# End of the feed-forward block: column groups of 6, 8, 8 and a second half that starts with the weights still on chip

## The chip, the cores and the metric

The kernel runs on one core of one Trainium2 chip. Its time is the device time of one execution in microseconds (us); lower is better. The core's engines run side by side and each works through its own queue in order: TensorE (PE in the rows, PEld for its weight loads), VectorE (DVE), ScalarE (ACT), GpSimd (POOL), and SyncE (SP), which here only issues DMAs.

## The reference

The program is a trunk of four layers over 512 token columns of width 1024: 256 context columns ("half 0") and 256 latent columns ("half 1"). Each layer has a mixer (kinds 0, 1, 2, 0) and then a feed-forward block (FFN). Before and after each there is an RMS norm with scales and shifts ("mods") that come from a small matrix product of a condition vector with `w_mod`. What the change touches is the FFN:

```python
def conv_ffn(h, w_in, conv_w, conv_b, w_out):
    u = dwconv_centred(h @ w_in, conv_w, conv_b)
    a, v = jnp.split(u, 2, axis=-1)
    return (jax.nn.silu(a) * v) @ w_out

h_l = rmsnorm(lat, norm_g[i, 2]) * (1.0 + m_l[4]) + m_l[3]
lat = lat + m_l[5] * rmsnorm(conv_ffn(h_l, ...), norm_g[i, 3])
```

`h @ w_in` gives 2 x 2816 rows, that is 22 pairs (a, v) of 128 rows; `w_out` takes the 22 gated rows of 128 back to 1024, that is 8 output groups of 128. In the last layer only half 1 is computed.

## The kernel before, in words

**Products in three matmuls.** An f32 product is made from split operands: `hi` is the value rounded to the matmul's format, `lo` the remainder. `mm3` (L680) issues three matmuls per k-chunk of 128: hi x hi (L688), lo x hi (L689), hi x lo (L690). Weights come as raw tiles `wraw` of up to 128 x 2048 by DMA and are split on the chip: ACT writes `whi` (L112, two instructions), DVE writes `wlo` (L115, two or more). `Stream` holds the list of weight tiles in program order. There are two raw buffers and two split buffers. `get` hands out the next split tile and, with `lead` 1, puts the split of the following one on a list; `mm3` issues one step of that list after every second k-chunk. Each split puts one raw load on SP's queue.

**The FFN** (`ffn`, L863). The 22 pairs are worked in three column groups, `FSPLIT`. In each group the pairs come first: a pair is 2 x 8 k-chunks of matmuls on `h` (48 matmuls of 512 columns), then ACT and DVE make the gated values `gh`, `gl` (lines 883 to 895). Then come the 8 output groups m = 0..7, each summing over the pairs of that column group only; two output groups share one weight tile ("fo", 256 x pairs columns). The results of the three column groups are added up in `y`. The first two output groups first run all pairs but the last three (`FS`) each, so that the gates of the last pair have time. In the last column group the output groups run once per half, with 256 columns: first all eight for half 0, then all eight for half 1, and before the change the four weight tiles are loaded and split again for half 1.

**What runs in between.** After the last output group of a half, `chain` (L492) is started: sum of squares (matmuls with `ones`, L446), square root on ACT, reciprocal on DVE, the update of `x`, a second norm, and the next layer's `h`. It is a generator; `mm3` advances it at k = 2 and k = 6 (`FT`). The chain of half 0 thus runs beside the output groups of half 1, and its instructions stand between theirs in every queue. Two further jobs are spread over the FFN. `s5_prep` (L1459, layers 0 and 1) prepares matrices of layer 2's mixer with small products (L1510) and, two advances later, transposes (L1538); it also advances with the k-chunks. `mod_block` (L300) makes a block of mods from two `wm` tiles (matmuls L314, then L383) and then has the next block's two tiles loaded (`mod_load`, L290); only one block is held on chip. `mod_slot` (L403) is called before each pair and after every second output group of the first two column groups, and runs a block when the count of slots passed says that one is due:

```python
m[3] += 1
if self.mod_nd < m[0] + min(m[1], -(-m[1] * m[3] // m[2])):
    self.mod_block()
```

So the last slot of a column group (after m = 7) and the first slot of the next (before its first pair) have no matmul between them. In layer 2 the mods are made on DVE instead.

**The FFN ends.** Layers 0 and 2 end as described (`tail` 0). In layer 1 the next mixer is of kind 2; its last pair is also done once per half (`tail` 1). Layer 3 has half 1 alone, so all its matmuls there have 256 columns.

Of the kernel before, what the change touches and what calls it, by code (L numbers as in the profile page):

```python
# [13 lines left out]
KINDS = (0, 1, 2, 0)  # L14
D = 1024
NK = 8
T = 512
NJ = 22
FSPLIT = (8, 7, 7)
FHEAD, FTAIL = (2, 1)  # L20
DM = 1
CW = (1, 8, 6)
# [24 lines left out]
FS = 3  # L47
# [34 lines left out]
class Stream:  # L82
# [10 lines left out]
    def add(self, key, ap, n):  # L93
        self.plan.append((key, ap, n))
# [57 lines left out]
class Kern:  # L152
# [688 lines left out]
    def plan_ffn(self, l, halves):  # L841
        tail = FTAIL if l < 3 and KINDS[l + 1] == 2 else 0
        add = self.ws.add
        fi = lambda j: add(("fi", l, j), self.a["f_w_in"][l * NJ + j], 2048)
        fo = lambda p, nj: [add(("fo", l, p, m), self.a[f"fo{p}"][l * 4 + m], 256 * nj) for m in range(NK // 2)]
        j0 = 0
        for p, nj in enumerate(FSPLIT):
            n0 = j0
            if p == 0 and len(halves) == 2:
                for j in [*range(FHEAD)] * (1 if FHEAD == 2 else 2):  # L850
                    fi(j)
                n0 = FHEAD
            last = p == len(FSPLIT) - 1
            t0 = j0 + nj - (tail if last else 0)
            for j in range(n0, t0):
                fi(j)
            for _ in range(2 if last and len(halves) == 2 else 1):
                for j in range(t0, j0 + nj):
                    fi(j)
                fo(p, nj)  # L860
            j0 += nj

    def ffn(self, l, halves, nxt):  # L863
        nc, tc = self.nc, self.tc
        both = len(halves) == 2
        allh = None if both else halves[0]
        tail = FTAIL if l < 3 and KINDS[l + 1] == 2 else 0
        cw0, cb0 = VEC["cw"][0] + l * 132, VEC["cb"][0] + l * 44
        rng = lambda half: (0, T) if half is None else RNG[half]
        with tc.tile_pool(name="ffn", bufs=1) as fp:  # L870
# [27 lines left out]
            def pair(j, half, G, ticks, w=None, defer=False):  # L898
                if w is None:
                    w = self.pairw(("fi", l, j))[0]  # L900
                ps = [self.proj(w[c], half, ticks) for c in range(2)]
                if j not in G:
                    G[j] = [fp.tile([128, T], F32R, name=n, bufs=max(FSPLIT)) for n in ("gh", "gl")]
                a, b = rng(half)
                run = lambda: act(j, ps, G[j][0][:, a:b], G[j][1][:, a:b])
                if defer:
                    return run
                run()

            j0 = 0  # L910
            for p, nj in enumerate(FSPLIT):
                G = {}
                n0 = j0
                if p == 0 and both:
                    ws = []
                    for half in halves:
                        for j in range(FHEAD):
                            if FHEAD == 2 and half == 0:
                                self.ws.lead = 1 - j
                                ws.append(self.pairw(("fi", l, j))[0])  # L920
                                self.ws.lead = 1
                            post = pair(j, half, G, None, ws[j] if ws else None,
                                        DF and half == 0 and j == FHEAD - 1)
                            if FHEAD == 2 and half and j == 0:
                                self.ws.prefetch()
                        self.drain(DM if half == 0 else 0)
                        if post:
                            post()
                    n0 = FHEAD
                if p == 0 and 2 in KINDS and l < 2:  # L930
                    self.bg = self.s5_prep(fp, 8 * l, 8 * l + 8)
                t0 = j0 + nj - (tail if p == len(FSPLIT) - 1 else 0)
                self.von, self.vpool = l in VO, fp
                for j in range(n0, t0):
                    if l not in VO:
                        self.mod_slot()
                    pair(j, allh, G, (3, 7))
                last = p == len(FSPLIT) - 1
                if last:
                    self.von = False  # L940
                self.cols = last and nxt is None
                if last and nxt is not None:
                    self.mod_until(nxt[0], 0)
                elif last:
                    self.mod_until(l, 5)
                for half in (halves if last else (allh,)):
                    a, b = rng(half)
                    for j in range(t0, j0 + nj):
                        pair(j, half, G, None)
                    self.flush()  # L950
                    for m in range(NK):
                        if m == 6 and last and nxt is not None and half == halves[-1] and KINDS[nxt[0]] == 2:
                            self.ws.lead = 0
                        if m % 2 == 0:
                            w = [t[:, :256 * nj].rearrange("p (c k m) -> p c k m", c=2, k=nj)
                                 for t in self.ws.get(("fo", l, p, m // 2))]
                        if m == 6 and last and nxt is not None and half == halves[-1] and KINDS[nxt[0]] == 2:
                            self.s5_pre = [self.s5_load("wraw", self.s5_h(i)) for i in range(2)]
                        g = lambda k: [G[j0 + k][z][:, a:b] for z in range(2)]
                        ticks = FT if last else (2, nj - 1)  # L960
                        if m < 2 and FS:
                            if m == 0:
                                two = [self.acc()[:, :b - a] for _ in range(2)]
                                for i in range(2):
                                    self.mm3(two[i], [t[:, i] for t in w], g, nj - FS, ticks, True, False)
                            ps = two[m]
                            self.mm3(ps, [t[:, m, nj - FS:] for t in w], lambda k: g(nj - FS + k), FS,
                                     [k - nj + FS for k in ticks], False, True)
                        else:
                            ps = self.acc()[:, :b - a]  # L970
                            self.mm3(ps, [t[:, m % 2] for t in w], g, nj, ticks)
                        if not last and m % 2 and l not in VO:
                            self.mod_slot()
                        if last and m == 3:
                            nc.scalar.activation(self.np_.tile([128, 8], F32, name="rs", bufs=4)[:, :1], self.epsc, AF.Sqrt)
                        y, ps = self.Y(m, half, ps)
                        if p == 0:
                            nc.scalar.activation(y, ps, AF.Copy)
                        else:
                            nc.vector.tensor_tensor(y, ps, y, op=ADD)  # L980
                        if last:
                            self.sq_add(("y", half), m, y)
                    if last:
                        self.drain()
                        self.gens.append(self.chain(l, 3, half, nxt))
                j0 += nj
# [943 lines left out]
```

## Time and profile before

| what | value |
|---|---|
| time, median of 3 runs | 2921.64 us (2917.19 to 2922.3) |
| the profiled execution's own time | 2920.22 us |
| its span, first to last instruction | 2918.4 us |
| busy: PE, DVE, ACT, POOL | 94%, 68%, 44%, 7% of the span |
| granted TensorE clock, mean | 0.969 of full speed |

The span is nearly all of the execution: 1.8 us lie outside it. A row's idle time, in square brackets, is the time for which the engine stood still just before the instruction, with the one that released it behind the arrow. In the windows view PEclk is the granted clock as a share of full speed: 1.00 is 2.4 GHz and 0.50 is 1.2 GHz.

### The profile page before, as it was taken

To read this page: it belongs to the slowest core of one execution; us is meant where nothing else is said; L and a number is where in the kernel's file an instruction comes from. 1 tells how busy PE (TensorE), PEld (TensorE's weight loads), DVE (VectorE), ACT (ScalarE), POOL (GpSimd) and SP (SyncE) were. 2 spreads that over 40 slices of the span, in tenths; PEclk is the share of its full clock that TensorE was granted. 3 is DMA by queue.
4 is the path that set the end of the run, shared out by engine and by line. 5 is a ranking of instruction groups with operands and counts; after the bars stand their busy time and mean duration, and the time that the engine had idled before them with its cause. 6 is when DMAs were issued, how large, how long until landed. Compare 5 with 4: busy or idle time off the path is not lost.

```text
span 2918.4 us, 53174 instructions
## 1 busy us (share of the span) xinstructions
PE 2740.2 (94%) x21814; PEld 2267.2 (78%) x21814; DVE 1992.1 (68%) x4405; ACT 1290.1 (44%) x2154; POOL 194.9 (7%) x192
## 2 busy tenths in 40 slices
PE   8999998999999999899999877989999989998998
PEld 5787776877788777777777745778888877887998
DVE  5775768766557655687564766378687876777776
ACT  4333334634335545553333565454332463433554
POOL 0000001122101000012110010010000010000000
PEclk9999999999999999999999988899999999999999
DMA  6232232355524343235555387433334453332553
GB/s 260 88 112 93 102 99 76 131 178 178 172 93 150 104 164 109 102 123 191 199 180 178 125 228 251 150 120 132 137 124 147 143 179 126 120 124 95 186 182 124
DMA packets 127043, 421.26 MB, mean 144 GB/s; under 512 B 36048, under 2 KB 55760, under 8 KB 102096
## 3 DMA queue, kind: packets, MB, share of 16 engines
q1 hardware_dynamic: 118608, 391.64, 39.5%
q0 software_dynamic: 5472, 23.07, 2.3%
q8 instruction: 172, 2.82, 0.4%
q10 hardware_dynamic: 2720, 3.15, 0.3%
q14 instruction: 71, 0.58, 0.1%
HBM read 392.78 MB, written 29.23 MB: 145 GB/s over the span
## 4 chain that ended last, share of the span: by engine, by line
PE 72%; DVE 16%; ACT 5%; DMA 3%; issue 2%; SPq 1%; POOL 0%; ACTq 0%; DVEq 0%; POOLq 0%
PE acc L688 19%; PE acc L689 18%; PE acc L690 17%; DVE wlo L115 3%; PE aux L314 2%; PE aux L1103 2%; PE acc L724 2%; PE acc L726 1%; PE acc L725 1%; DVE bc L462 1%; DVE y L561 1%; ACT whi L112 1%; PE aux L1143 1%; PE aux L383 1%; DVE y L520 1%
## 5 line engine op out<-in xcount | busy, mean ns | idle before, releaser
L688 PE MATMUL acc<-h,whi 128*128 128x512 f32 (+1 forms) x2368 | 868.3, 367 | 24.8 <-ACT h L574 15.3
L689 PE MATMUL acc<-h,whi 128*128 128x512 f32 (+1 forms) x2368 | 842.7, 356 | 19.4 <-DVE h L581 17.0
L690 PE MATMUL acc<-h,wlo 128*128 128x512 f32 (+1 forms) x2368 | 837.8, 354 | 2.3 <-DVE wlo L115 2.3
L115 DVE TENSOR_TENSOR wlo<-wraw,whi 128x512 fp32r<-128x512 f32 (+5 forms) x674 | 601.7, 920 | 153.0 <-ACT whi L112 152.6
L688 PEld LDWEIGHTS acc<-h,whi 128*128 128x128 f32 x2368 | 458.6, 194 | 94.1 <-ACT h L574 18.2
L689 PEld LDWEIGHTS acc<-h,whi 128*128 128x128 f32 x2368 | 458.9, 194 | 80.0 <-DVE h L581 24.3
L112 ACT ACTIVATE whi<-wraw 128x1024 fp32r<-128x1024 f32 (+3 forms) x496 | 479.5, 1014 | 66.6 <-PE acc L689 51.7
L690 PEld LDWEIGHTS acc<-h,wlo 128*128 128x128 f32 x2368 | 458.8, 194 | 62.1 <-DVE wlo L115 3.2
L688 PE MATMUL acc<-gh,whi 128*128 128x256 f32 (+1 forms) x872 | 294.7, 338 | 8.6 <-ACT gh L894 8.6
L689 PE MATMUL acc<-gl,whi 128*128 128x256 f32 (+1 forms) x872 | 287.2, 329 | 0.8 <-DVE gl L895 0.7
L690 PE MATMUL acc<-gh,wlo 128*128 128x256 f32 (+1 forms) x872 | 287.1, 329 | 0.0
L883 ACT ACTIVATE u<-acc,vec 128x512 f32<-128x512 f32 (+1 forms) x190 | 129.6, 692 | 254.5 <-PE acc L690 254.3
L886 DVE SCALAR_TENSOR_TENSOR u<-acc,vec,u 128x510 f32<-128x510 f32 (+1 forms) x190 | 122.2, 643 | 113.2 <-ACT u L883 113.0
L688 PEld LDWEIGHTS acc<-gh,whi 128*128 128x128 f32 x872 | 164.8, 189 | 25.6 <-ACT gh L894 9.0
L689 PEld LDWEIGHTS acc<-gl,whi 128*128 128x128 f32 x872 | 164.7, 189 | 16.8 <-DVE gl L895 1.7
L690 PEld LDWEIGHTS acc<-gh,wlo 128*128 128x128 f32 x872 | 164.6, 189 | 15.9
L1074 DVE TENSOR_TENSOR FB<-FB,P 128x256 f32<-128x256 f32 x384 | 145.2, 421 | 31.9 <-PE aux L1103 29.3
L887 DVE SCALAR_TENSOR_TENSOR u<-acc,vec,u 128x510 f32<-128x510 f32 (+1 forms) x190 | 123.1, 648 | 6.7
L724 PE MATMUL acc<-whi,h 128*128 128x256 f32 x384 | 115.2, 300 | 2.2 <-ACT whi L112 1.2
L894 ACT ACTIVATE gh<-u 128x512 fp32r<-128x512 f32 (+1 forms) x95 | 52.3, 551 | 144.1 <-DVE u L893 144.1
L726 PE MATMUL acc<-wlo,h 128*128 128x256 f32 x384 | 110.0, 287 | 4.1 <-DVE wlo L115 4.1
L725 PE MATMUL acc<-whi,h 128*128 128x256 f32 x384 | 109.7, 286 | 0.0
(298 smaller groups left out, 3957.2 us busy)
## 6 DMA issues: line engine op xcount, KB each, us to landing
wm<-in_w_mod SPq DMA_DIRECT2D x192, 512.0 KB, 5.3
wraw<-in_f_w_in SPq DMA_DIRECT2D x89, 1024.0 KB, 4.9
wraw<-in_fo SPq DMA_DIRECT2D x44, 896.0 KB, 4.6
wraw<-in_a_qz SPq DMA_DIRECT2D x18, 1024.0 KB, 4.9
wraw<-in_a_zg SPq DMA_DIRECT2D x18, 1024.0 KB, 4.9
wraw<-in_fo SPq DMA_DIRECT2D x16, 1024.0 KB, 4.9
wraw<-in_a_v SPq DMA_DIRECT2D x15, 1024.0 KB, 4.9
wraw<-in_c_glu SPq DMA_DIRECT2D x12, 1024.0 KB, 4.8
```

The source lines that it names most:

```text
L112: nc.scalar.activation(hi[:, a:b], r[:, a:b], AF.Copy)
L115: nc.vector.tensor_tensor(lo[:, a:b], r[:, a:b], hi[:, a:b].bitcast(F32), op=SUB)
L688: nc.tensor.matmul(ps, wh[:, k], hh, start=(first and k == 0), stop=False, **kw)
L689: nc.tensor.matmul(ps, wh[:, k], hl, start=False, stop=False, **kw)
L690: nc.tensor.matmul(ps, wl[:, k], hh, start=False, stop=(last and k == nk - 1), **kw)
L724: nc.tensor.matmul(o, hh, wh[:, :, k, :], start=(k == 0), stop=False)
L725: nc.tensor.matmul(o, hl, wh[:, :, k, :], start=False, stop=False)
L726: nc.tensor.matmul(o, hh, wl[:, :, k, :], start=False, stop=(k == NK - 1))
L883: nc.scalar.activation(u, ps[c], AF.Identity, scale=w(1), bias=self.vec[:, cb0 + ch:cb0 + ch + 1])
L886: nc.vector.scalar_tensor_tensor(u3[:, :, 1:], p3[:, :, :255], w(0), u3[:, :, 1:], op0=MUL, op1=ADD)
L887: nc.vector.scalar_tensor_tensor(u3[:, :, :255], p3[:, :, 1:], w(2), u3[:, :, :255], op0=MUL, op1=ADD)
L1074: nc.vector.tensor_tensor(o, o, p, op=MUL)
```

## The change

`FSPLIT` becomes (6, 8, 8): the first column group has 6 pairs instead of 8, the other two 8 instead of 7. In the FFN ends of layers 0 and 2 (`again`) half 1 takes its output groups in the order 4, 5, 6, 7, 2, 3, 0, 1: the first four use the two split weight tiles that half 0 used last, and only the tiles of 2, 3 and of 0, 1 are loaded and split again. To keep the two tiles, no split is started in half 0's last two output groups (`lead` 0), and splitting starts again at half 1's third.

```diff
--- before.py
+++ after.py
@@ -16,7 +16,7 @@
 NK = 8
 T = 512
 NJ = 22
-FSPLIT = (8, 7, 7)
+FSPLIT = (6, 8, 8)
 FHEAD, FTAIL = (2, 1)
 DM = 1
 CW = (1, 8, 6)
@@ -842,7 +842,7 @@
         tail = FTAIL if l < 3 and KINDS[l + 1] == 2 else 0
         add = self.ws.add
         fi = lambda j: add(("fi", l, j), self.a["f_w_in"][l * NJ + j], 2048)
-        fo = lambda p, nj: [add(("fo", l, p, m), self.a[f"fo{p}"][l * 4 + m], 256 * nj) for m in range(NK // 2)]
+        fo = lambda p, nj, ms: [add(("fo", l, p, m), self.a[f"fo{p}"][l * 4 + m], 256 * nj) for m in ms]
         j0 = 0
         for p, nj in enumerate(FSPLIT):
             n0 = j0
@@ -854,10 +854,10 @@
             t0 = j0 + nj - (tail if last else 0)
             for j in range(n0, t0):
                 fi(j)
-            for _ in range(2 if last and len(halves) == 2 else 1):
+            for i in range(2 if last and len(halves) == 2 else 1):
                 for j in range(t0, j0 + nj):
                     fi(j)
-                fo(p, nj)
+                fo(p, nj, (1, 0) if i and not tail else range(NK // 2))
             j0 += nj
 
     def ffn(self, l, halves, nxt):
@@ -948,30 +948,41 @@
                     for j in range(t0, j0 + nj):
                         pair(j, half, G, None)
                     self.flush()
-                    for m in range(NK):
-                        if m == 6 and last and nxt is not None and half == halves[-1] and KINDS[nxt[0]] == 2:
+                    again = last and both and not tail
+                    for i, m in enumerate((4, 5, 6, 7, 2, 3, 0, 1) if again and half else range(NK)):
+                        if i == 6 and last and (again and not half or
+                                                nxt is not None and half == halves[-1] and KINDS[nxt[0]] == 2):
                             self.ws.lead = 0
-                        if m % 2 == 0:
+                        if again and half and i == 2:
+                            self.ws.lead = 1
+                            self.ws.prefetch()
+                        if again and half and i in (0, 2):
+                            w = kept.pop(0)
+                        elif m % 2 == 0:
                             w = [t[:, :256 * nj].rearrange("p (c k m) -> p c k m", c=2, k=nj)
                                  for t in self.ws.get(("fo", l, p, m // 2))]
-                        if m == 6 and last and nxt is not None and half == halves[-1] and KINDS[nxt[0]] == 2:
+                            if m == 4:
+                                kept = []
+                            if m > 3:
+                                kept.append(w)
+                        if i == 6 and last and nxt is not None and half == halves[-1] and KINDS[nxt[0]] == 2:
                             self.s5_pre = [self.s5_load("wraw", self.s5_h(i)) for i in range(2)]
                         g = lambda k: [G[j0 + k][z][:, a:b] for z in range(2)]
                         ticks = FT if last else (2, nj - 1)
-                        if m < 2 and FS:
-                            if m == 0:
+                        if i < 2 and FS:
+                            if i == 0:
                                 two = [self.acc()[:, :b - a] for _ in range(2)]
-                                for i in range(2):
-                                    self.mm3(two[i], [t[:, i] for t in w], g, nj - FS, ticks, True, False)
-                            ps = two[m]
-                            self.mm3(ps, [t[:, m, nj - FS:] for t in w], lambda k: g(nj - FS + k), FS,
+                                for c in range(2):
+                                    self.mm3(two[c], [t[:, c] for t in w], g, nj - FS, ticks, True, False)
+                            ps = two[i]
+                            self.mm3(ps, [t[:, i, nj - FS:] for t in w], lambda k: g(nj - FS + k), FS,
                                      [k - nj + FS for k in ticks], False, True)
                         else:
                             ps = self.acc()[:, :b - a]
                             self.mm3(ps, [t[:, m % 2] for t in w], g, nj, ticks)
                         if not last and m % 2 and l not in VO:
                             self.mod_slot()
-                        if last and m == 3:
+                        if last and i == 3:
                             nc.scalar.activation(self.np_.tile([128, 8], F32, name="rs", bufs=4)[:, :1], self.epsc, AF.Sqrt)
                         y, ps = self.Y(m, half, ps)
                         if p == 0:
@@ -979,7 +990,7 @@
                         else:
                             nc.vector.tensor_tensor(y, ps, y, op=ADD)
                         if last:
-                            self.sq_add(("y", half), m, y)
+                            self.sq_add(("y", half), i, y)
                     if last:
                         self.drain()
                         self.gens.append(self.chain(l, 3, half, nxt))
```

What this does to the queues, at three places. First PE in layer 1, at the border between the first two column groups; `wm` are the mods' weight tiles, `gh`/`gl` the gated values, `h` the input of the next pair. Before:

```order
L688 MATMUL acc<-gh,whi 128x512
L689 MATMUL acc<-gl,whi 128x512
L690 MATMUL acc<-gh,wlo 128x512
L314 MATMUL aux<-wm,sT 32x256 x8
L383 MATMUL aux<-sel,mev 128x2 x2
L688 MATMUL acc<-h,whi 128x512
L689 MATMUL acc<-h,whi 128x512
L690 MATMUL acc<-h,wlo 128x512
L688 MATMUL acc<-h,whi 128x512
```

and now:

```order
L688 MATMUL acc<-gh,whi 128x512
L689 MATMUL acc<-gl,whi 128x512
L690 MATMUL acc<-gh,wlo 128x512
L314 MATMUL aux<-wm,sT 32x256 x8
L383 MATMUL aux<-sel,mev 128x2 x2
L314 MATMUL aux<-wm,sT 32x256 x8
L383 MATMUL aux<-sel,mev 128x2 x2
L688 MATMUL acc<-h,whi 128x512
L689 MATMUL acc<-h,whi 128x512
L690 MATMUL acc<-h,wlo 128x512
L688 MATMUL acc<-h,whi 128x512
```

A second block of mods now stands directly behind the first; at the border between the second and third column groups of layer 1 the same four L314/L383 rows stand between `gh` and `h` matmuls. There are 81 blocks in both kernels.

Second PE in layer 0, in the seventh output group of half 1; `y,ones` are the chain's sums for half 0, `sl,ones` a sum of squares of half 1. Before:

```order
L688 MATMUL acc<-gh,whi 128x256
L689 MATMUL acc<-gl,whi 128x256
L690 MATMUL acc<-gh,wlo 128x256
L446 MATMUL aux<-y,ones 128x256 x3
L446 MATMUL aux<-sl,ones 128x256
L688 MATMUL acc<-gh,whi 128x256
L689 MATMUL acc<-gl,whi 128x256
L690 MATMUL acc<-gh,wlo 128x256
L688 MATMUL acc<-gh,whi 128x256
```

and now:

```order
L690 MATMUL acc<-gh,wlo 128x256
L446 MATMUL aux<-y,ones 128x256 x3
L688 MATMUL acc<-gh,whi 128x256
L689 MATMUL acc<-gl,whi 128x256
L690 MATMUL acc<-gh,wlo 128x256
L446 MATMUL aux<-sl,ones 128x256
L688 MATMUL acc<-gh,whi 128x256
L689 MATMUL acc<-gl,whi 128x256
L690 MATMUL acc<-gh,wlo 128x256
```

The chain's sums now have one more k-chunk behind them in their own output group, and each following group has 24 matmuls instead of 21.

Third ACT in layer 0, from the end of half 0 to the third output group of half 1; `sq`, `bc` are squares of half 0, `sl` of half 1. Before:

```order
L484 ACTIVATE sq<-y 128x256
L484 ACTIVATE bc_8806<-y 128x256
L112 ACTIVATE whi<-wraw 128x896 x2
L460 ACTIVATE aux<-aux,epsc 128x256
L484 ACTIVATE sl<-y 128x256
L530 ACTIVATE y<-x 128x256
L484 ACTIVATE sl<-y 128x256
L112 ACTIVATE whi<-wraw 128x896
L530 ACTIVATE y<-x 128x256
L112 ACTIVATE whi<-wraw 128x896
```

and now:

```order
L484 ACTIVATE sq<-y 128x256 x3
L484 ACTIVATE bc_8798<-y 128x256
L460 ACTIVATE aux<-aux,epsc 128x256
L484 ACTIVATE sl<-y 128x256
L530 ACTIVATE y<-x 128x256
L484 ACTIVATE sl<-y 128x256
L112 ACTIVATE whi<-wraw 128x1024
L530 ACTIVATE y<-x 128x256
L112 ACTIVATE whi<-wraw 128x1024
L530 ACTIVATE y<-x 128x256
```

The split that stood between the last square of half 0 and the chain's square root (L460) is gone, and so is the one two rows further up; the one behind the second `sl` stays.

## Rows read from the trace of the kernel before

**Rows 1.** Page, part 4: shares of the chain that ended last, by engine
```profile
PE 72%; DVE 16%; ACT 5%; DMA 3%; issue 2%; SPq 1%; POOL 0%; ACTq 0%; DVEq 0%; POOLq 0%
```
**Rows 2.** Windows, pairs of layer 2's third column group: length, busy time and count by engine
```profile
core 0: us, PE busy (x) PEld busy (x) DVE busy (x) ACT busy (x) POOL busy (x), PEclk, DMA share, GB/s
2220.00:2295.00 75.00, 75.00 (x344) 62.50 (x343) 60.83 (x109) 27.65 (x37) 0.00 (x0) 1.00 0.39 131
```
**Rows 3.** Waits of PE, 872 to 928 us, layer 0's end: total us, times, longest
```profile
PE aux L446 <- ACT sl L484: 2.5, 3, 1.4
PE acc L689 <- DVE h L581: 1.6, 2, 0.9
PE acc L688 <- ACT h L574: 0.6, 1, 0.6
PE acc L689 <- DVE gl L895: 0.3, 1, 0.3
```
**Rows 4.** Waits of PE, 1643 to 1692 us, half 1 of layer 1's end
```profile
PE acc L688 <- ACT gh L894: 8.2, 1, 8.2
PE aux L446 <- ACT sl L484: 3.8, 3, 2.1
```
**Rows 5.** Waits of PE, 2295 to 2356 us, layer 2's end; squares and `gl` as in 3
```profile
...
PE acc L689 <- DVE h L581: 2.0, 3, 0.9
PE acc L688 <- ACT gh L894: 0.4, 1, 0.4
...
```
**Rows 6.** Timeline of PE, two mod blocks in a row: start, length, [idle]
```profile
416.92 0.64 PE L314 MATMUL aux<-wm,sT 128*32 128x256 f32 x8 [3.29 <-DMA wm<-in_w_mod]
418.06 1.08 PE L314 MATMUL aux<-wm,sT 128*32 128x256 f32 x8 [0.51 <-DMA wm<-in_w_mod]
```
**Rows 7.** Windows, the 10 us after that wait, columns as in group 2
```profile
418.00:428.10 10.10, 9.51 (x47) 8.61 (x48) 3.36 (x12) 4.49 (x8) 0.00 (x0) 0.50 0.35 106
```
**Rows 8.** DMA issues, 411 to 421 us: count, size, median from issue to landing
```profile
wm<-in_w_mod SPq DMA_DIRECT2D x4, 512.0 KB, 4.4
```
**Rows 9.** DMA issues, 1360 to 1520 us, layer 1's FFN
```profile
wm<-in_w_mod SPq DMA_DIRECT2D x20, 512.0 KB, 5.1
```
**Rows 10.** Timeline of SP, the slowest load of mod weights in layer 1
```profile
1542.04 2.29 SPq L296 DMA_DIRECT2D wm<-in_w_mod  x2
```
**Rows 11.** Timeline of PE, the block that uses that load
```profile
1552.33 0.64 PE L314 MATMUL aux<-wm,sT 128*32 128x256 f32 x8 [0.53 <-DMA wm<-in_w_mod]
```
**Rows 12.** Timeline of PE, first transposes of `s5_prep` in layer 0
```profile
588.00 0.55 PE L1538 MATMUL aux<-ident,W 128*128 128x128 f32 x3 [1.85 <-DVE W L1485]
588.31 0.63 PE L688 MATMUL acc<-h,whi 128*128 128x512 f32 x1
...
591.29 0.63 PE L689 MATMUL acc<-h,whi 128*128 128x512 f32 x1
```
**Rows 13.** Timeline of PE, 512-column matmuls on `gh`, layer 2
```profile
2213.03 0.40 PE L690 MATMUL acc<-gh,wlo 128*128 128x512 f32 x1
...
2216.51 0.41 PE L690 MATMUL acc<-gh,wlo 128*128 128x512 f32 x1
```
**Rows 14.** Timeline of PE, 256-column matmuls on `gh`, layer 3
```profile
2822.16 0.28 PE L690 MATMUL acc<-gh,wlo 128*128 128x256 f32 x1
...
2824.65 0.29 PE L690 MATMUL acc<-gh,wlo 128*128 128x256 f32 x1
```
**Rows 15.** Timeline of PE, transposes in layer 0's second column group
```profile
761.15 0.55 PE L1538 MATMUL aux<-ident,W 128*128 128x128 f32 x3 [0.74 <-DVE W L1485]
```
**Rows 16.** Timeline of PE, first `gh` matmul of layer 3's first column group
```profile
2755.18 0.28 PE L688 MATMUL acc<-gh,whi 128*128 128x256 f32 x1
```
**Rows 17.** Timeline of DVE, end of the gate of that column group's last pair
```profile
2758.80 0.43 DVE L895 TENSOR_TENSOR gl<-u,gh 128x256 fp32r<-128x256 f32 x1 [0.48 <-ACT gh L894]
```

## The prediction

> **What bounds the kernel now.** I read the chain that ended last first: 72% of it is TensorE, DVE comes second with 16% [rows 1]. So a saving counts only where PE stands still or does the work itself. Then the windows of a stretch inside the FFN, away from its ends: PE is busy in all 75 us of it at the full clock, VectorE in 61 [rows 2]. Nothing that ACT, DVE or the DMA queues are spared there is worth anything, and whatever stops PE there is paid in full. Then the waits of PE at the three FFN ends that the change re-orders. Layer 0 loses 5.0 us, the sum of its four rows [rows 3], layer 2 loses 5.2 us, 2.0 and 0.4 in rows of its own and again 2.5 and 0.3, which read as in layer 0 [rows 3, 5], and half 1 of layer 1 loses 8.2 us before its last pair's gate and 3.8 us for squares [rows 4]. These 22 us are what the change can win from; 8.2 of them belong to the chain of half 0, which keeps its length.
>
> **Regrouping, matmuls.** In layers 0 to 2 one pair moves from 512-column matmuls to two times 256 columns: 24 of the one become 48 of the other. One of 512 takes (2216.51 - 2213.03) / 15 = 0.232 us [rows 13], one of 256 (2824.65 - 2822.16) / 21 = 0.119 us [rows 14]. That is 24 x (2 x 0.1186 - 0.232) = +0.12 us a layer, +0.4 us in all. The Trainium skill (TensorE: Matmul & The Clock Gate, Back-to-back issue gap) gives about 131 ns a matmul at 512 columns and 81 ns at 128 in a sustained stream with weight loads, which speaks against halving the columns. By it two of 256 would cost at least 24 x (2 x 81 - 131) ns = 0.74 us more a layer, an estimate; the trace has 232 ns at 512 columns, so the measurement decides, and the 0.4 stays.
>
> **Regrouping, longer output groups.** The last column group now has 8 chunks: PE works 3 x 0.119 = 0.36 us longer on each output group while DVE, ACT and the chain have the same queue apart from splits 1/7 wider. Where PE waits, that work costs nothing, and the wait shrinks by it. (The work itself comes out of the earlier column groups, which is in the 0.4.) (a) Gate of the last pair: PE has 36 instead of 30 matmuls to do first, 0.71 us more. Layer 0's 0.3, layer 2's 0.4 + 0.3 and 0.71 of layer 1's 8.2 go: -1.7. (b) Waits for squares, L446: the first lies behind two longer groups, the two later ones behind one. That is 0.71 + 0.36 + 0.36 = 1.4 in each of layers 0 and 2, of the 2.5 that they have, and 3 x 0.36 = 1.1 in layer 1: -3.9. (c) Waits for the next layer's `h`: the chain's sums stand one chunk (3 matmuls) further from the end of their group, and one longer group follows. So PE arrives 6 x 0.119 = 0.71 us later: -1.4 over layers 0 and 2. Bounds for (a) to (c): zero where the chain is late by as much, and all 22 us less the 7.5 that layer 1's gate keeps, 14.7.
>
> **The kept tiles.** Layers 0 and 2 drop two loads, two splits on ACT and two on DVE each. The order shows where they stood: around the last squares of half 0 and in half 1's first two output groups. The splits beside the waits (third to eighth output group) are still there. PE waits at none of the removed ones, so I cost this at 0; the work that hides them is half 0's matmuls. The upper end of what it can win is the waits above.
>
> **Mods, the new wait.** This is a consequence of the regrouping that the diff does not name. Slots are counted per pair and per two output groups, so moving the borders moves which slot runs a block. In layer 1 blocks now fall on the last slot of a column group and on the first slot of the next, twice. The second block needs tiles whose load is issued only when the first has read the old ones. Queued behind it on PE are the next pair's matmuls, hence everything. Before has such a place elsewhere: PE stood 3.29 and 0.51 us [rows 6], with loads landing 4.4 us after their issue [rows 8]. In layer 1 the median is 5.1 us [rows 9], so 3.8 + 0.7 = 4.5 us each. Lower end 3.8. Upper end: one load there was issued at 1542.04 and released PE only at 1552.33 [rows 10, 11], 10.3 us, which makes 3.8 + 10.3 - 4.4 = 9.7 us each. The value is nearest to the median, as 20 loads stand behind it. At one matmul group's distance the wait was only 0.53 [rows 11], so the 0.53 may go as well; I leave it.
>
> After the wait of 3.29 us the granted clock was 0.50, that is 1.2 GHz, for the 10 us of the window [rows 7]; after a wait of 1.85 us 512-column matmuls ran at (591.29 - 588.31) / 7 = 0.426 us instead of 0.23 [rows 12], for 8 matmuls, a loss of 8 x 0.2 = 1.6 us. I add 1.6 to each place: the stretch behind it is dense matmul work, as in group 12; the far ends are 0 and 5 us (10 us at half rate). The Trainium skill (TensorE: Matmul & The Clock Gate, HAM oscillation — how this bites in real kernels) says that a wait for a DMA leaves the array at half rate, so that the next stretch starts cold. By that rule the two places cost 12.2 us, by the waits alone 9.0; the trace agrees with it in groups 6 and 7.
>
> So 2 x (4.5 + 1.6) = +12.2 us.
>
> **S5 preparation in layer 0.** The first transposes wait 1.85 us for DVE after 24 matmuls [rows 12]. Now the products stand at the same place and 18 matmuls of the first output groups follow: 6 x 0.232 = 1.4 us less cover, +1.4. The wait of 0.74 us in the second column group [rows 15] has 24 instead of 21 matmuls of cover, 0.7 us: -0.7. The same shortening in later rounds I put at 0, since these showed no wait (bounds -0.3 to +1.5).
>
> **Layer 3's first column group.** With 6 pairs only 24 matmuls of 256 columns come before the last pair's `gh` is read. They start at 2755.18 [rows 16], so `gl` would be needed at 2755.18 + 25 x 0.1186 = 2758.15 and is written at 2758.80 + 0.43 = 2759.23 [rows 17]: +1.1. In layers 0 to 2 the 24 have 512 columns and take 5.6 us, which with the S5 work between them covers the gate (0 to +1).
>
> **Sum.** +0.4 - 1.7 - 3.9 - 1.4 + 0 + 12.2 + 1.4 - 0.7 + 1.1 = +7.4 us. On the profiled execution's 2920.2 us (span 2918.4 and 1.8 outside) that is 2927.6; the median of the three runs is 1.4 us higher, so 2929.0 us.
>
> **Rivals.**
> 1. The double blocks don't stop PE: the loads land before PE reaches the second block. For it: 0.53 us was all that a load in flight cost at a distance of 42 matmuls [rows 11]. Against: here the distance is two small matmuls, and group 6 shows what that costs. Then the sum is 7.4 - 12.2 = -4.8: 2916.8 us, just inside no change.
> 2. Faster, through the kept tiles: without the removed splits, ACT and DVE finish half 0's chain before PE asks for anything, and the waits of groups 3 and 5 and the squares of group 4 go entirely. It decides if `h` of the next layer is written before PE has done its last sum of squares. Price: -14.7 instead of the -7.0 of (a) to (c); with waits of 3.8 and no slow clock, 7.6 + 0.4 + 0.7 + 1.1 - 14.7 = -4.9, and up to -3 more where the clock no longer falls: 2914 to 2917 us. Against: the splits that go are not those beside the waits.
> 3. Heavier: at both borders the strided S5 copies and weight loads share the DMA queues, loads take 10.3 us as in groups 10 and 11, and the clock stays at half rate for 10 us: 2 x (9.7 + 5) = 29.4 instead of 12.2, 2946 us.
> That the reuse does nothing is part of the forecast already.
>
> **Chances.** Forecast 0.55, rival 1 0.20, rival 2 0.12, rival 3 0.13. The forecast's own range is 2923 (waits of 3.8, no slow clock) to 2936 (waits of 6, 3 us of clock each). The range for 8 in 10 takes in most of rival 1 and part of 3: 2916 to 2940. A measurement of this kernel can tell 0.2% from no change, 5.8 us: above 2927.5 is slower, below 2915.8 faster. Slower: most of the forecast (0.45) and rival 3 (0.13), 0.58. Same: the forecast's low part (0.10), rival 1 (0.15), the rest of rival 2 (0.03), 0.28. Faster: 0.14.
>
> **What would show it.** Right: two rows L314 in layer 1's FFN with 3 to 6 us idle, released by the `wm` load, and PEclk 0.50 behind them; about 1 us idle for `gl` at layer 3's first output groups; waits of PE for L484 in layers 0 and 2 near 1 us each; 3 us idle at the first L1538 of layer 0. Wrong: L314 without idle time there, or the waits at the ends of layers 0 and 2 gone altogether, or a wait of the third output group for its re-split tile. The forecast falls if the double blocks cost under 3 us each.

## The result and the profile after

The changed kernel takes 2937.98 us (median; 2935.31 to 2939.16) against 2920.56 us before on the same chip. The ratio is 1.0060, with a 95% interval of 1.0046 to 1.0074: slower by 17 us where the forecast was 7. Its profiled execution took 2939.05 us, with a span of 2937.2 us, 18.8 us above that of before. The chain that ended last shifts a little towards TensorE, from 72% to 74% of the span [rows 1].

Where the 18.8 us are is read from eight windows: the FFNs of layers 0 to 3, each to its last `gh` matmul (layer 2's from its first 512-column matmul, layer 3's to the end), and what lies ahead of and between them. Five of them in after, columns as in group 2; the first, third and fourth row are the FFNs of layers 0, 1 and 2:

```profile
493.30:926.00 432.70, 420.49 (x2603) 346.28 (x2604) 292.51 (x509) 186.97 (x298) 56.88 (x48) 0.98 0.42 143
926.00:1246.30 320.30, 303.33 (x1976) 240.69 (x1974) 196.37 (x431) 162.43 (x346) 13.41 (x16) 0.96 0.34 122
1246.30:1708.50 462.20, 439.57 (x2767) 358.85 (x2768) 293.51 (x483) 189.05 (x305) 58.22 (x51) 0.96 0.48 163
2000.20:2368.60 368.40, 362.70 (x1824) 307.75 (x1823) 275.21 (x493) 134.27 (x189) 5.28 (x6) 1.00 0.38 137
2368.60:2720.40 351.80, 320.11 (x3448) 274.85 (x3446) 257.74 (x608) 153.66 (x255) 14.30 (x14) 0.97 0.36 126
```

In before the eight stages took 492.4, 430.3, 322.1, 445.3, 291.5, 365.8, 354.6 and 216.4 us; the three of after that are not shown, the first, the fifth and the last, took 493.3, 291.7 and 216.8. The differences are +0.9, +2.4, -1.8, **+16.9**, +0.2, +2.6, -2.8 and +0.4, in sum +18.8. Nearly all of it is layer 1's FFN. The +0.9 stands ahead of the first changed instruction. That stretch took 494.6 us in the trace of after_slots24 and 495.8 in that of split_778 (both below), so 2 or 3 us of one stage in one trace prove nothing by themselves.

In layer 1's FFN PE comes to the first border of column groups with two mod blocks in a row. Timeline of PE, after: start, length, [idle and what ended it]; the rows L689 and L690 are the next pair's matmuls.

```profile
1376.04 1.07 PE L314 MATMUL aux<-wm,sT 128*32 128x256 f32 x16
1377.05 0.61 PE L383 MATMUL aux<-sel,mev 128*128 128x2 f32 x4
1383.49 2.23 PE L314 MATMUL aux<-wm,sT 128*32 128x256 f32 x16 [5.84 <-DMA wm<-in_w_mod]
1385.66 1.01 PE L383 MATMUL aux<-sel,mev 128*128 128x2 f32 x4
...
1387.11 0.63 PE L689 MATMUL acc<-h,whi 128*128 128x512 f32 x1
1387.53 0.63 PE L690 MATMUL acc<-h,wlo 128*128 128x512 f32 x1
...
1551.26 2.25 PE L314 MATMUL aux<-wm,sT 128*32 128x256 f32 x16 [4.20 <-DMA wm<-in_w_mod]
```

The second block's 16 matmuls take 2.23 us where the first block's took 1.07, and the pair's matmuls follow each other in 0.43 us instead of 0.23. That is the granted clock. Windows of after behind the two waits:

```profile
1383.50:1391.80 8.30, 8.23 (x32) 5.38 (x33) 5.05 (x7) 2.27 (x3) 1.44 (x1) 0.50 0.40 140
1551.30:1559.10 7.80, 7.72 (x31) 5.02 (x32) 2.69 (x4) 2.28 (x3) 0.00 (x0) 0.50 0.39 143
```

PE is busy in both and both run at 0.50, that is 1.2 GHz. Half of 8.23 + 7.72 us is lost: 8.0 us. With the waits of 5.84 + 4.20 us, less the 0.53 us that before had there [rows 11], the two places cost 17.5 us.

The ends of the FFNs, waits of PE in after: layer 0 (871 to 932 us), then half 1 of layer 1 (1637 to 1710), then layer 2 (2308 to 2378).

```profile
PE aux L446 <- ACT sl L484: 2.4, 3, 0.9
PE acc L689 <- DVE h L581: 2.1, 3, 0.9
...
PE aux L446 <- DVE y L476: 3.5, 1, 3.5
PE aux L446 <- ACT sl L484: 3.0, 3, 1.5
PE acc L688 <- ACT gh L894: 1.4, 1, 1.4
...
PE aux L446 <- ACT sl L484: 2.4, 3, 0.9
PE acc L690 <- DVE wlo L115: 1.7, 1, 1.7
PE acc L689 <- DVE h L581: 1.4, 2, 0.7
PE aux L380 <- DVE mac L335: 1.4, 1, 1.4
PE acc L689 <- DVE gl L895: 0.2, 1, 0.2
```

Against [rows 3 to 5]: the waits for squares in layers 0 and 2 stay at 2.4 of 2.5 us. Half 1 of layer 1 idles 7.9 us instead of 12.0, but more of its work ran at half clock. The stretch at 0.50 beside these waits, first in before, then in after:

```profile
1660.30:1667.10 6.80, 3.15 (x8) 2.56 (x9) 4.92 (x9) 5.39 (x7) 0.00 (x0) 0.50 0.00 0
1675.20:1688.80 13.60, 9.87 (x33) 8.15 (x34) 10.51 (x19) 9.38 (x15) 0.00 (x0) 0.50 0.21 78
```

Half of PE's busy time in it is lost, 4.9 us instead of 1.6. So of the 4.1 us that the waits fell only about 0.8 was won. Layer 2 has two waits that were not there, 1.7 us for a split weight tile and 1.4 us for mods that DVE computes. Layer 0's first column group has others, answering to [rows 12], where it lost 2.0 us in all. Waits of PE in after, 578 to 600 us:

```profile
PE acc L688 <- ACT gh L894: 2.6, 1, 2.6
PE aux L1549 <- DVE W L1496: 1.6, 1, 1.6
PE acc L690 <- DVE wlo L115: 1.2, 1, 1.2
```

The wait of [rows 15] is gone. In layer 3, `gl` arrives just late [rows 16, 17]: the matmul that needs it starts 0.45 us behind the one ahead (at 2765.37) instead of 0.12, a loss of 0.3 us.

### The profile page after: what moved, and what is told of

Same layout as the page of the kernel before. It is cut to its first block, busy times and chain, and to the rows that moved or that the text cites. A ratio compares the mean times of both kernels' runs of the same rounds, so it can differ in the third digit from the quotient of the medians.

```text
span 2937.2 us, 53301 instructions
## 1 busy us (share of the span) xinstructions
PE 2746.6 (94%) x21886; PEld 2272.9 (77%) x21886; DVE 1988.4 (68%) x4397; ACT 1286.2 (44%) x2146; POOL 189.1 (6%) x192
## 4 chain that ended last, share of the span: by engine, by line
PE 74%; DVE 14%; ACT 5%; DMA 3%; issue 2%; SPq 1%; POOL 0%; ACTq 0%; DVEq 0%; POOLq 0%
PE acc L688 19%; PE acc L689 18%; PE acc L690 18%; DVE wlo L115 3%; PE aux L314 2%; PE aux L1114 2%; PE acc L724 2%; PE acc L726 1%; PE acc L725 1%; DVE bc L462 1%; DVE y L561 1%; ACT whi L112 1%; PE aux L1154 1%; PE aux L383 1%; PE aux L446 1%
## 5 line engine op out<-in xcount | busy, mean ns | idle before, releaser
L689 PE MATMUL acc<-h,whi 128*128 128x512 f32 (+1 forms) x2368 | 840.6, 355 | 20.3 <-DVE h L581 17.5
L690 PE MATMUL acc<-h,wlo 128*128 128x512 f32 (+1 forms) x2368 | 836.0, 353 | 2.3 <-DVE wlo L115 2.3
L115 DVE TENSOR_TENSOR wlo<-wraw,whi 128x512 fp32r<-128x512 f32 (+4 forms) x666 | 595.6, 923 | 134.6 <-ACT whi L112 133.8
L689 PEld LDWEIGHTS acc<-h,whi 128*128 128x128 f32 x2368 | 457.5, 193 | 80.3 <-DVE h L581 24.5
L690 PEld LDWEIGHTS acc<-h,wlo 128*128 128x128 f32 x2368 | 457.2, 193 | 62.3 <-DVE wlo L115 2.9
L112 ACT ACTIVATE whi<-wraw 128x1024 fp32r<-128x1024 f32 (+1 forms) x488 | 473.8, 1018 | 71.9 <-PE acc L689 57.5
L690 PE MATMUL acc<-gh,wlo 128*128 128x256 f32 (+1 forms) x896 | 292.6, 327 | 2.9 <-DVE wlo L115 2.9
L689 PE MATMUL acc<-gl,whi 128*128 128x256 f32 (+1 forms) x896 | 293.2, 327 | 0.7 <-DVE gl L895 0.4
L883 ACT ACTIVATE u<-acc,vec 128x512 f32<-128x512 f32 (+1 forms) x190 | 129.5, 692 | 260.4 <-PE acc L690 260.2
L688 PEld LDWEIGHTS acc<-gh,whi 128*128 128x128 f32 x896 | 170.8, 191 | 21.4 <-ACT gh L894 6.1
L690 PEld LDWEIGHTS acc<-gh,wlo 128*128 128x128 f32 x896 | 170.5, 190 | 18.3 <-DVE wlo L115 3.6
L689 PEld LDWEIGHTS acc<-gl,whi 128*128 128x128 f32 x896 | 170.6, 190 | 16.8 <-DVE gl L895 2.8
L724 PE MATMUL acc<-whi,h 128*128 128x256 f32 x384 | 115.0, 300 | 2.2 <-ACT whi L112 1.3
L314 PE MATMUL aux<-wm,sT 128*32 128x256 f32 x1312 | 93.0, 400 | 20.1 <-DMA wm<-in_w_mod 19.9
```

Of the source, the lines that this page charges most:

```text
L112: nc.scalar.activation(hi[:, a:b], r[:, a:b], AF.Copy)
L115: nc.vector.tensor_tensor(lo[:, a:b], r[:, a:b], hi[:, a:b].bitcast(F32), op=SUB)
L314: nc.tensor.matmul(ps[32 * j:32 * j + 32, :256], self.sT[:, k, :], r[q][:, j, :], start=(q == 0), stop=(q == 1), tile_position=(0, 32 * j))
L688: nc.tensor.matmul(ps, wh[:, k], hh, start=(first and k == 0), stop=False, **kw)
L689: nc.tensor.matmul(ps, wh[:, k], hl, start=False, stop=False, **kw)
L690: nc.tensor.matmul(ps, wl[:, k], hh, start=False, stop=(last and k == nk - 1), **kw)
```

## The experiments

Each ratio is to the kernel before, run on the same chip (medians there 2920.38 us for after_slots24, before_slots24, keep_only and split_only, 2919.71 for after_filled18 and split_778, 2920.53 for the rest).

**after_slots24 and before_slots24.** The same edit to both kernels. In after it takes the double blocks away (slots 8 and 20, the last ones of the first two column groups, then run no block), in before it makes two (blocks on slots 10 and 11 and on 21 and 22, either side of a border).

```diff
-                self.mod_plan(nxt[0], 0, 22, VX[l])
+                self.mod_plan(nxt[0], 0, 24 if l == 1 else 22, VX[l])
```

> The changed kernel with layer 1's 18 mod blocks spread over 24 slots instead of 22, so that none of them stands back to back with the next; all else as after. Theory (the two double blocks carry the loss): their waits of 5.84 and 4.20 us go, and with them the half clock behind each, which I put at 4.2 us a place from the after trace (24 matmuls in 8.20 us instead of 5.6, 16 small mod matmuls in 2.24 instead of 1.07, four more in 1.01 instead of 0.61). Together 10.0 + 8.4 = 18.4 us off 2938.0: 2919.6 us, L314 without idle time in layer 1. Rival A (the second half and the borders of the other layers carry half of it): only the 10 us of waits go, the clock falls all the same at some other stop: 2928 us. Rival B (the loads themselves are late, wherever the blocks stand): waits of 2 to 4 us stay at single blocks, 2930 us or more.

> The kernel before, with the same single edit (24 slots instead of 22 in layer 1), which puts two blocks back to back at both borders there; column groups 8, 7, 7 and the second half stay as before. Theory (double blocks): two L314 rows with 4 to 6 us idle released by the wm load and half clock behind each: +18 us, 2938 to 2939 us. Rival A: about +10 us, 2931 us. If the loss belongs to the column groups or to the kept tiles, nothing moves: 2920.6 us.

Measured: after_slots24 2920.11 us, ratio 0.9997 (0.9988 to 1.0006); before_slots24 2933.29 us, ratio 1.0039 (1.0026 to 1.0053). So without the double blocks the change costs nothing, and with them the kernel before loses 13 us. Waits of PE in layer 1's FFN, of after_slots24 (1286 to 1691 us), where no wait for `wm` is left:

```profile
PE aux L446 <- ACT sl L484: 3.9, 3, 2.3
PE aux L446 <- DVE y L476: 3.2, 1, 3.2
PE acc L688 <- ACT gh L894: 2.3, 1, 2.3
```

The same view of before_slots24 (1286 to 1706 us), then its windows behind the two waits:

```profile
PE acc L688 <- ACT gh L894: 8.2, 1, 8.2
PE aux L314 <- DMA wm<-in_w_mod: 7.7, 4, 3.8
PE aux L446 <- ACT sl L484: 3.8, 3, 2.0
```

```profile
1417.00:1425.40 8.40, 8.24 (x33) 5.40 (x34) 4.49 (x7) 2.27 (x3) 0.66 (x1) 0.50 0.47 142
1562.00:1569.00 7.00, 7.00 (x24) 5.14 (x25) 2.69 (x4) 2.27 (x3) 0.00 (x0) 0.51 0.51 162
```

Here 7.7 us of waits and half of 15.2 us at half clock make 15.3, less the 0.53 of before 14.8. The time rose by 12.9, with an interval of 7.6 to 15.5. Rival A's 10 us lie in that interval too; it is after_slots24 that refutes it. I had expected 18, having taken after's longer waits. The loads that PE waits for landed 7.0 and 5.4 us after their issue in after (median of the two tiles of each) and 5.0 and 4.5 us in before_slots24, so a double block has no fixed price.

**keep_only and split_only.** Each does one half of the change: keep_only is after with the old column groups (the edit below), split_only is before with the new ones (the same lines the other way).

```diff
-FSPLIT = (6, 8, 8)
+FSPLIT = (8, 7, 7)
```

> The second half with its two kept weight tiles, with column groups 8, 7, 7 as before. Theory: the splits that go were not waited for, so 0 to -2 us: 2918.6 to 2920.6 us. Rival C (the kept tiles free ACT and DVE in time for the squares and gates of the second half): -5 us, 2915.5 us. Rival D (the other order of the output tiles makes the last squares late or the re-split tile is waited for): +3 us, 2923.5 us, with a wait for whi or wlo at the third or fourth output group of half 1.

> Column groups 6, 8, 8 with the second half as before (four output tiles loaded and split again). Theory: it has both double blocks, so nearly the whole loss: 2937 to 2940 us. Rival C: without the kept tiles it is 5 us worse than after, 2943 us. Rival D: it is 3 us better than after, 2935 us. If the kept tiles carry the loss, it is at 2922 us.

Measured: keep_only 2919.67 us, ratio 0.9999 (0.9990 to 1.0008); split_only 2937.20 us, ratio 1.0060 (1.0046 to 1.0074), as after. The kept tiles are worth nothing that can be measured, in either grouping. In keep_only half 1 of layer 1 waits as before, 8.5 us for the gate and 3.9 us for squares.

**after_filled and after_filled18.** These keep the double blocks and give PE something to do between the two. After_filled18 has 18 in place of 34.

```diff
+                    if l == 1 and p and j == n0:
+                        ps = self.aux()
+                        for _ in range(34):
+                            nc.tensor.matmul(ps[:, :128], self.ident, self.ident, start=True, stop=True)
                     if l not in VO:
                         self.mod_slot()
```

> The changed kernel with its two double blocks kept, and 34 small matmuls (identity by identity, 128 columns, result not read) between the two blocks of each, about 4.8 us of work at the 0.14 us that such a matmul takes at full clock; the load that is waited for is issued before them, as before. Theory (wait and half clock are two costs that add up, 10.0 and 8.1 us in the trace of after): PE now works through the wait instead of standing still, the second block still starts some 4.2 to 5.8 us late, but the granted clock stays at 1.0 behind both: 2937.98 - 8 + up to 1 = 2930 to 2931 us, with idle time under 1.5 us at L314. Rival A (the half clock is not tied to the idle time): PEclk 0.50 again behind both places, 2937 to 2939 us. Rival B (the double blocks disturb by their loads, not by the wait): the matmuls behind stay slow, 2938 us.

> As after_filled, with 18 instead of 34 small matmuls between the two blocks: at the 0.23 us that one took there (7.84 us for 34) they are 4.15 us, so they should end before the loads land and add nothing to the waits of after (5.84 and 4.20 us), while PE stands still for at most 2 us. Theory (wait and half clock are two costs): the 10.0 us of waits stay, as work or as idle time, and the 8.1 us of half clock go: 2938.0 - 8.1 = 2930 us; in after_filled the filling was longer than the waits, 7.84 + 0.58 and 7.84 us for 10.04, which gave 2935.4. Rival A (a rest of 1 to 2 us of idle time is enough for the clock to fall): PEclk 0.50 behind the first place, 2933 to 2934 us. Rival B (what after_filled gained over after is chance): 2937 to 2938 us.

Measured: after_filled 2935.38 us, ratio 1.0056 (1.0043 to 1.0068); after_filled18 2934.49 us, ratio 1.0055 (1.0041 to 1.0068). In after_filled I had sized the filling wrongly, by a matmul of 0.14 us that takes 0.23: 7.84 us stood at each place, more than the waits that they replaced. But the clock stayed. Windows of after_filled behind the two places:

```profile
1388.20:1396.50 8.30, 8.30 (x82) 6.54 (x82) 5.50 (x8) 2.71 (x5) 2.50 (x2) 1.00 0.38 130
1554.00:1562.00 8.00, 8.00 (x37) 6.63 (x37) 4.08 (x6) 3.06 (x4) 0.00 (x0) 1.00 0.74 257
```

The two places cost 7.84 + 0.58 + 7.84 = 16.3 us there against 18.0 in after, so 1.8 us less by the rows. The medians differ by 2.6 us, which is within the noise. After_filled18 tells more, since its places differ. Timeline of PE in after_filled18 (the L938 rows are the filling), then its windows behind each:

```profile
1377.02 4.26 PE L938 MATMUL aux<-ident 128*128 128x128 f32 x36
1383.34 0.64 PE L314 MATMUL aux<-wm,sT 128*32 128x256 f32 x8 [2.05 <-DMA wm<-in_w_mod]
1384.60 1.08 PE L314 MATMUL aux<-wm,sT 128*32 128x256 f32 x8 [0.62 <-DMA wm<-in_w_mod]
...
1545.28 4.26 PE L938 MATMUL aux<-ident 128*128 128x128 f32 x36
1550.05 0.64 PE L314 MATMUL aux<-wm,sT 128*32 128x256 f32 x8 [0.51 <-DMA wm<-in_w_mod]
1551.41 0.64 PE L314 MATMUL aux<-wm,sT 128*32 128x256 f32 x8 [0.72 <-DMA wm<-in_w_mod]
```

```profile
1384.60:1391.20 6.60, 6.60 (x23) 4.82 (x24) 4.51 (x6) 2.27 (x3) 1.44 (x1) 0.50 0.51 159
1552.00:1559.80 7.80, 7.80 (x40) 6.54 (x37) 3.43 (x5) 3.06 (x4) 0.00 (x0) 1.00 0.68 224
```

At the first place 2.67 us of standing still were left, and the clock fell all the same; at the second 1.23 us were left, and it did not. That is rival A, by its row, 0.50 behind the first place. The time excludes the theory's 2930 us, but it does not tell rival A from rival B, chance: the interval of after, 1.0046 to 1.0074, overlaps with both here. So it is the rows that show the half clock to be a cost of its own, tied to PE standing still, which the load alone does not bring; that the kernel became faster without it is not shown. The Trainium skill (TensorE: Matmul & The Clock Gate, HAM oscillation — how this bites in real kernels) says of a kernel with long enough waits for DMAs that each next stretch starts cold; the first place agrees with it at 0.50, and the second, at 1.00 behind waits of 0.51 and 0.72 us, shows waits for a DMA that did not do it.

**slots24_fs1.** After_slots24 with more cover for the last pair's gate.

```diff
-FS = 3
+FS = 1
```

> As after_slots24 (2920.1 us), with FS = 1 instead of 3: the first two output groups of a column group hold back only their last chunk, so 30 instead of 24 matmuls come before the gate of the last pair is read where a group has 6 chunks, and 42 instead of 36 where it has 8. Theory (in layer 0's first column group PE is short of cover: waits of 1.23, 1.64 and 2.55 us): the wait for gh of 2.55 us shrinks by 6 x 0.23 = 1.4 us, layer 1's second gate (2.33) by 6 x 0.12 = 0.7: 2918 us, which is below what can be told from 2920 by the time, so the rows decide. Rival (DVE's queue is what is late, and the matmuls that now come first need wlo or the S5 weights earlier): the wait moves to wlo (1.23 grows) and the sum stays, 2920 us.

Measured: 2929.31 us, ratio 1.0034 (1.0021 to 1.0046): slower by 9 us, which neither theory had. Layer 0's gate still waits (2.5 us): the wait for the split tile went, PE came there earlier by it, and the six more matmuls (1.4 us) only took up that. And the squares of the second half got dearer. Waits of PE in half 1 of layer 1 (1640 to 1698 us), where after_slots24 has 4.5, 3.2 and 2.3 for L446 twice and the gate:

```profile
PE aux L446 <- ACT sl L484: 7.6, 2, 7.0
PE aux L446 <- DVE y L476: 4.0, 1, 4.0
```

The gate's wait is gone there, and one of 7.0 us for squares has come. Why it is so long I did not follow further. The waits alone are not the 9 us: here they sum to 11.6 us instead of 10.0, and in layer 2's end one of 3.3 us stands where after_slots24 has three that sum to 2.4. The mean granted clock of the profiled execution was 0.965 instead of 0.968, and 0.003 of 2918 us is 9 us, so by this estimate the larger part goes with the clock.

**keep_868, keep_778 and split_778.** Other places for the long group, with 20 slots in layer 1 so that no blocks stand in a row; keep_778 has (7, 7, 8) in the first edited line, and split_778 has these numbers with the second half as before.

```diff
-FSPLIT = (6, 8, 8)
+FSPLIT = (8, 6, 8)
-                self.mod_plan(nxt[0], 0, 22, VX[l])
+                self.mod_plan(nxt[0], 0, 20 if l == 1 else 22, VX[l])
```

> The kept tiles with column groups 8, 6, 8 and 20 slots in layer 1, which leaves no double block there. Layer 0's first column group has its 8 pairs again. Theory: the new waits of layer 0's first group (1.22 and 2.56 us) go and 6 chunks stand where no S5 rush is on, so 2.5 to 4 us better than after_slots24: 2916 to 2918 us. Rival (what the first group loses comes back in the second, where S5 work also runs): 2920 us, with waits for gh and wlo of the same size there.

> The kept tiles with column groups 7, 7, 8 and 20 slots in layer 1, no double block there. Theory: layer 0's first group loses one pair of cover instead of two, half of the 3.4 us: 2918 us. Rival: as for 8, 6, 8: 2920 us.

> Column groups 7, 7, 8 and 20 slots in layer 1, with the second half as before (no kept tiles): tells whether the 3.6 us that keep_778 has on before belong to the column groups and slots or to the kept tiles. If to the groups (the removal of the 0.5 us at L314, shorter waits at layer 1's end, no rush in layer 0's first group): 2917 to 2918 us. If to the kept tiles: 2920 to 2921 us.

Measured: keep_868 2922.35 us, ratio 1.0003 (0.9994 to 1.0012); keep_778 2916.91 us, ratio 0.9990 (0.9981 to 0.9998); split_778 2916.34 us, ratio 0.9986 (0.9977 to 0.9994). Keep_868 missed its theory: with six pairs second, the gate's wait moves to the second group (1.7 us at 747 us), as the rival said, though no wait for `wlo` came with it. With seven pairs first, the first group has none, as the theory of keep_778 said, and the second 0.3 us. From 578 to 605 us PE waits 2.0 us in split_778, all of it for the first transposes, as in before. Split_778 is faster than both kernels, by 0.14% against before. Keep_778 is no better than it, so the kept tiles have no part in the gain; what of it is due to the groups and what to the slots was not taken apart.

## Why the prediction was right and wrong

Right were the direction, the cause and its place: two double blocks in layer 1, which the diff does not name. By the runs they are all of the loss (2937.98 - 2920.11 = 17.9 us). The size was off by 10 us, in four steps. The time is above the forecast's own range, which ended at 2936; it lies in the wide one, up to 2940, because that took in part of rival 3, and for the size this is luck. By stages of the profiled executions, forecast and measured: layer 0's FFN -0.9 and +2.4, layer 1's +10.5 and +16.9, layer 2's -2.0 and +2.6, the stages behind layers 0 and 2 together -1.4 and -4.6, layer 3 +1.1 and +0.4.

- **Mods, the new wait.** The waits were forecast at 9.0 us and measured at 10.0; the two loads that PE waits for landed 7.0 and 5.4 us after their issue instead of 5.1. The clock was mis-sized: "I add 1.6 to each place" took the 8 slow matmuls behind a wait of 1.85 us [rows 12]. The row of the same situation was the other one, a wait of 3.29 us for the same load with 10 us at 0.50 behind it [rows 7]. It gives 5 us a place, which I had kept as the far end; 4.0 were measured. Terms: 12.2 forecast, 17.5 measured.
- **S5 preparation and "covers the gate (0 to +1)".** The 3 us at the first transposes did not come (1.6). Instead PE waits before them for `wlo` (1.2) and behind them for the last pair's `gh` (2.6): 5.4 us against 2.0, +3.4 instead of +1.4. I counted PE's cover, 24 matmuls, and not DVE's queue. The gate's work on DVE stands behind the S5 weights in it. Timeline of DVE in after: the last S5 step, then the first and the last step of that pair's gate.

```profile
588.23 0.23 DVE L1540 SCALAR_TENSOR_TENSOR kk<-s5c,kk 128x16 f32<-128x16 f32 x1
588.38 0.74 DVE L886 SCALAR_TENSOR_TENSOR u<-acc,vec,u 128x510 f32<-128x510 f32 x1
...
592.84 0.69 DVE L895 TENSOR_TENSOR gl<-u,gh 128x512 fp32r<-128x512 f32 x1 [0.69 <-ACT gh L894]
```

- **Longer output groups.** (a) Of the gates, layer 0's 0.3 us went as forecast, and in layer 1 the wait of 8.2 became 3.5 + 1.4, 3.3 us less instead of 0.7; but the longer half clock beside it took 3.3 us back (4.9 less 1.6), and the sum had no term for that. In layer 2 0.5 of the 0.7 went, and 1.7 + 1.4 came: 2.46 us of `mac`, mods computed on DVE, stand ahead of the split that PE needs there, and PE's sums of mods (L380, 1.2 us), which in before ran ahead of the output group that needs this split, now come behind it. (b) failed: -3.9 forecast, and the waits for squares fell by 0.1 in layers 0 and 2 and 0.8 in layer 1. In layer 2 two of before's three waits did shrink (1.37 to 0.77 us, 0.45 to none), but a new one of 0.93 us came where PE had not waited. "PE works 3 x 0.119 = 0.36 us longer" was taken as pure cover, with splits 1/7 wider as an aside. But DVE is busy 14.1 of the 16.1 us from 2345.0 to 2361.1, PE 13.7: DVE sets the pace, and two of these splits stand in its queue ahead of the `y` (L991) whose squares PE awaits from 2351.9 to 2352.84. In before the second split stands behind that `y`: `mm3` issues a step of a split after every second chunk, so a group of 8 chunks puts all four steps of one ahead of its `y`, a group of 7 only three. Timeline of DVE at layer 2's end, in before, then in after:

```profile
2330.09 1.09 DVE L115 TENSOR_TENSOR wlo<-wraw,whi 128x896 fp32r<-128x896 f32 x1 [0.59 <-ACT whi L112]
2331.11 0.42 DVE L526 TENSOR_TENSOR x<-x,y 128x256 f32<-128x256 f32 x1
2331.44 0.42 DVE L980 TENSOR_TENSOR y<-acc,y 128x256 f32<-128x256 f32 x1
2331.78 1.08 DVE L115 TENSOR_TENSOR wlo<-wraw,whi 128x896 fp32r<-128x896 f32 x1
...
2349.30 1.23 DVE L115 TENSOR_TENSOR wlo<-wraw,whi 128x1024 fp32r<-128x1024 f32 x1 [0.70 <-ACT whi L112]
2350.45 0.42 DVE L526 TENSOR_TENSOR x<-x,y 128x256 f32<-128x256 f32 x1
2350.78 1.22 DVE L115 TENSOR_TENSOR wlo<-wraw,whi 128x1024 fp32r<-128x1024 f32 x1
2351.92 0.42 DVE L991 TENSOR_TENSOR y<-acc,y 128x256 f32<-128x256 f32 x1
```

- **(c)** was right in sign. The waits for `h` fell from 2.2 to 2.1 us in layer 0 and from 2.0 to 1.4 in layer 2, so the mechanism is seen in layer 2 alone. But the stages behind layers 0 and 2 gained 1.8 and 2.8 us against 0.7 each. With the same 3448 matmuls PE is busy 320.1 instead of 324.1 us behind layer 2, so in after what was gained there is matmul speed. Measured to the first gate step (L883) of the next FFN, the stage behind layer 2 takes 362.2 us in before, 362.5 in keep_only and 360.0 in split_only, so its gain goes with the groups; that behind layer 0 takes 339.9, 338.2 and 338.1, so its gain comes with either half of the change. Each of these is one execution, and why is open.

The small terms held or came out smaller. PE's busy time in layer 2's FFN rose from 362.5 to 362.7 us (+0.1 forecast), the 0.74 us of the second group went, and layer 3 cost 0.3 instead of 1.1. The kept tiles are 0, as forecast. Without the mods the sum was -4.8; after_slots24 shows -0.3, with an interval of -3.5 to +1.8.

Of the rivals, 1 is refuted by the waits of 5.84 and 4.20 us and 2 by keep_only, at 0.9999. Rival 3 was wrong in its mechanism (the waits were 5.84 and 4.20 us, not 9.7) and nearly right in its clock (5 us a place, 4.0 measured): with the forecast's waits and 4 us of clock a place, the sum would have been 2 x (4.5 + 4.0) - 4.8 = +12.2, and most of the rest is the 4.5 us that the ends did not give back.

## What to carry to other kernels

Work that is dealt out by counting loop slots moves when the loop's borders move: print the order and look for two uses of a single buffer in a row, and retune the count with the borders (22 to 24 here was worth 17.9 us). A wait on TensorE can cost nearly as much again at half clock: behind waits of 3.3 to 5.8 us for mod weights here, 6 to 10 us of work ran at 0.50 and 3 to 5 us were lost, while the 8.2 us at layer 1's end in before lost only 1.6 more. So give the clock a term of its own beside every wait that comes, goes or moves, and take it from the row of the situation most like it. Before a longer matmul group is booked as cover, read the queue of the engine that is waited for: where DVE sets the pace, wider tiles lengthen both sides.

## What the runs showed of the hardware

Matmuls whose result nobody reads kept the granted clock at 1.00 where a wait of 4.20 us had been followed by 0.50 (after_filled18, second place: 4.26 us of such matmuls, 1.23 us of idle time left). They do not shorten the wait, and a gain in the kernel's time is not shown. A small matmul of identity by identity, 128 columns in f32, took 0.23 us in a stream of them (after_filled, 7.84 / 34).
